# A decoder layer on one core: the first weight sum of the down projection moves ahead of its stage, its first split to the head of each chunk, and the last two token blocks close one by one

## The chip, the cores and the metric

The kernel runs on one core of one Trainium2 chip. The metric is the device time of one execution in microseconds (us), the median of several runs. TensorE is called PE, VectorE DVE, ScalarE ACT, GpSimd POOL and SyncE SP. SP and POOL are used here mainly as the two queues that issue transfers; only POOL's transfers add into their destination.

## The reference

One decoder layer over 512 tokens with a model width of 1024, all in float32. The change touches only the second half, the convolutional gated feed-forward network, and the projection just ahead of it:

```python
h = h + rmsnorm(merged @ w_out, mix_post_g)          # end of the mixer
xn = rmsnorm(h, ffn_pre_g)
hid = xn @ w_up                                      # 1024 -> 2 * 2816
conv = conv_b + sum_j shifted(hid, j) * conv_w[j]    # three taps along the sequence
a, u = split(conv, 2)
y = (gelu(a) * u) @ w_down                           # 2816 -> 1024
out = h + rmsnorm(y, ffn_post_g)
```

## The kernel before

**Precision.** Every float32 operand is split into a rounded high part and a low part (`split`, or `weights` for a matrix that comes from memory), and each product is three matmuls: high by high, high by low, low by high. `weights` issues a load on SP into a tile `wraw`, ACT makes the high part (line 98) and DVE the low part (line 99). The three tags `wraw`, `whi` and `wlo` have three buffers each, so at most three weight matrices are anywhere between their load and their last matmul. Up weights show in the trace as `h_wup` and `l_wup`, plain blocks of the down weights as `h_db` and `l_db`.

**Up projection.** The loop over `f` runs over the 22 blocks of 128 hidden channels. Each `f` has two weight matrices (the gate channel and the value channel), each with 24 matmuls of 512 columns into a PSUM bank of tag `acc`. `gate_up` then runs the convolution (ACT line 846, DVE line 848), the gelu and the gate, and prepares the operands of the down projection.

**Down projection.** It works in five chunks of 512 hidden channels, `c` 0 to 4; two more blocks of 128 remain and are multiplied plainly at the end (`close`). Chunk `c` is worked on during the up projection of `f = 4c+4` to `4c+7`. Within a chunk a 2 by 2 block product is done with seven block products in place of eight (Strassen's scheme with Winograd's sums). Four of its weight operands are sums of weight blocks, named t1 (T1 in the text), T2, T3 and T4 in the code, and three are plain blocks: b21, b11 and b22. A product over one block is 12 matmuls.

T1, T2 and T4 come out of one tile `dr`: SP loads block (0,1), POOL adds block (0,0), which gives T1. `parts` splits T1 into the pair `dht`, `dlt` (lines 853 and 854) and then has POOL add a further block into the same tile (line 910), which gives T2; splitting T2 starts the last addition, which gives T4. T3 has its own tile `dt`. Before the change `dr` has two buffers in the pool `ffn`, which opens after the mixer's pools have closed, and `sums` asks for both tiles at `f = 4c+2`.

**Order.** The program text is a list of priorities for the Tile framework: it lets an instruction go ahead of earlier ones on its engine when it counts it ready sooner and a buffer is free, and then fixes one order for each engine. At run time each engine and each queue keeps to its own order, and an instruction that waits holds up all that stand behind it on its engine. `steps` (chunks 0 to 3) and `last` (chunk 4) are generators: `go(cur)` runs one to its next `yield`, once ahead of the up matmuls of each `f` and once behind them. In the text before, the weights of chunk `c` are asked for in this order: up 4c+4 (two), b21, b11, up 4c+5 (two), T1, and so on.

**End.** The 512 tokens are four blocks `n` of 128, each with two column halves. `close(n, hf)` adds the two remaining blocks, `summed` adds the bank to the accumulator and starts the sum of squares, `finish(n)` computes the reciprocal root (POOL, `r2o`), scales, adds the residual and stores. Blocks 2 and 3 still lack the products S3·T3 and A22·T4 when blocks 0 and 1 are finished.

Of the kernel before, what the change touches and what calls it, by code (L numbers as in the profile page):

```python
# [9 lines left out]
F32 = mybir.dt.float32  # L10
# [3 lines left out]
ALU = mybir.AluOpType  # L14
PSUM = bass.MemoryType.PSUM

P = 128
S = 512
# [48 lines left out]
def hybrid_layer_kernel(ctx: ExitStack, tc: tile.TileContext, a):  # L67
    nc = tc.nc
# [144 lines left out]
    with ExitStack() as mix:  # L213
# [79 lines left out]
        for i in range(2):  # L293
            proj_fm(a["w_gq"][i], f"wgq{i}", lambda pq, i=i: nc.vector.scalar_tensor_tensor(
                out=gq[:, i, :], in0=pq, scalar=0.125, in1=rsb, op0=ALU.mult, op1=ALU.mult))
        for i in range(2):
            proj_fm(a["w_gk"][i], f"wgk{i}", lambda pk, i=i: nc.vector.tensor_tensor(
                out=gk[:, i, :], in0=pk, in1=rsb, op=ALU.mult))
# [40 lines left out]
        for gp in range(4):  # L339
# [4 lines left out]
            for gg in range(2):  # L344
                g = 2 * gp + gg
                c = slice(g * 64, (g + 1) * 64)
                nc.vector.scalar_tensor_tensor(
                    out=u_t[:, :, c], in0=sp[:, gg * 256:(gg + 1) * 256].rearrange("p (n d) -> p n d", d=64),
# [103 lines left out]
        for i in range(2):  # L452

            ups = [bank("att", f"up{i}{e}") for e in range(2)]
            for c in range(7):
                n, r = c // 2, (c % 2) * 64
# [245 lines left out]
        def gain(name):  # L702
            g = late.tile([P, D], F32, tag="gain", bufs=2, name=name)
            nc.gpsimd.dma_start(out=g, in_=a[name].broadcast_to([P, D]))
            nc.gpsimd.tensor_scalar(out=g, in0=g, scalar1=32.0, scalar2=1.0, op0=ALU.mult, op1=ALU.mult)
            return g
# [2 lines left out]
        nc.gpsimd.dma_start(out=cw, in_=a["ffn_conv_w"])  # L709
        cb = const.tile([P, 2 * KF], F32, name="cb")  # L710
        nc.gpsimd.dma_start(out=cb, in_=a["ffn_conv_b"])
        gpost = gain("mix_post_g")
        gpre = gain("ffn_pre_g")

        with tc.tile_pool(name="mlo", bufs=1, side="right") as mlp:
# [58 lines left out]
            def out_part(n, u, hf, w):  # L774
                hi, lo = w
                t = slice(n * P, (n + 1) * P)
                for j in range(2):
                    k = 2 * u + j
                    mm3(bs[n][hf], mh[:, k, t], ml[:, k, t], hi[:, j, :], lo[:, j, :], k == 0, k == KD - 1)
# [5 lines left out]
            for u in range(2):  # L785
                for hf in range(2):
                    w = weights(a["w_out"][u, hf], [2, S], f"wo{u}{hf}")
                    for n in range(NB):
                        out_part(n, u, hf, w)
            for hf in range(2):  # L790
                wo[2, hf] = weights(a["w_out"][2, hf], [2, S], f"wo2{hf}", (keep[0][:, hf], keep[1][:, hf]))
            for hf in range(2):
# [46 lines left out]
    NCH = 5  # L839
# [18 lines left out]
    def gate_up(f, pa, pu):  # L858
# [12 lines left out]
        if f % 2 == 0:  # L871
# [13 lines left out]
        nc.vector.scalar_tensor_tensor(out=l[:, S2, :], in0=sm[:, 3, :], scalar=-1.0,  # L885
                                       in1=h[:, S2, :].bitcast(F32), op0=ALU.mult, op1=ALU.subtract)

    class Down:


        def __init__(self, c):
            self.c, self.w = c, a["ffn_w_down"][c]
            self.bank = {}

        def sums(self):

            c, w = self.c, self.w
            self.r = ffn.tile([P, 2, S], F32, tag="dr", bufs=2, name=f"dr{c}")
            nc.sync.dma_start(out=self.r, in_=w[0, 1])
            nc.gpsimd.dma_start(out=self.r, in_=w[0, 0], accum_op=ALU.add)  # L900
            self.t3 = ffn.tile([P, 2, S], F32, tag="dt", bufs=1, name=f"dt{c}")
            nc.sync.dma_start(out=self.t3, in_=w[1, 1])
            nc.gpsimd.dma_start(out=self.t3, in_=w[0, 1], accum_op=ALU.add)

        def parts(self, x, name, then=None):
            hi = ffn.tile([P, 2, S], F32R, tag="dh", bufs=2, name=f"dh{name}{self.c}")
# [6 lines left out]
        def plain(self, r, s_, name):  # L913
            return weights(self.w[r, s_], [2, S], f"d{name}{self.c}")

        def product(self, tag, blk, w, start, stop):
            hi, lo = w
            for tau in range(2):
                key = (tag, tau)
                if start:  # L920
                    self.bank[key] = bank(tag, f"dn{tag}{self.c}{tau}")
                out = self.bank[key]
                t = slice(tau * P, (tau + 1) * P)
                for j in range(2):
                    h, l = halves[2 * self.c + j]
                    mm(out, h[:, blk, t], hi[:, j, :], start=start and j == 0, stop=False, skip_group_check=True)  # L926
                    mm(out, h[:, blk, t], lo[:, j, :], start=False, stop=False, skip_group_check=True)  # L927
                    mm(out, l[:, blk, t], hi[:, j, :], start=False, stop=stop and j == 1, skip_group_check=True)  # L928
# [8 lines left out]
                    nc.vector.tensor_tensor(out=dst, in0=src, in1=dst, op=ALU.add)  # L937

        def steps(self):
            b21 = self.plain(1, 0, "b21")  # L940
            yield
            self.product("tv", A12, b21, True, True)
            self.add("tv", 0, 0, True)
            b11 = self.plain(0, 0, "b11")
            yield
            t1 = self.parts(self.r, "t1", self.w[1, 1])
            yield
            self.product("att", A11, b11, True, False)
            self.add("att", 0, 0)
            self.add("att", 1, 0, True)  # L950
            self.product("att", S1, t1, False, False)
            self.add("att", 1, 1, True)
            yield
            T2, b22 = self.parts(self.r, "t2", self.w[1, 0]), self.plain(1, 1, "b22")
            yield
            self.product("tv", S2, T2, True, False)
            self.add("tv", 0, 1, True)
            self.product("att", S4, b22, False, True)
            self.add("att", 0, 1)
            yield  # L960
            T3, T4 = self.parts(self.t3, "t3"), self.parts(self.r, "t4")
            yield
            self.product("tv", S3, T3, False, False)
            self.add("tv", 1, 1)
            self.product("tv", A22, T4, False, True)
            self.add("tv", 1, 0)

        def last(self):

            b11 = self.plain(0, 0, "b11")  # L970
            yield
            self.product("att", A11, b11, True, False)
            self.add("att", 0, 0)
            self.add("att", 1, 0)
            t1 = self.parts(self.r, "t1", self.w[1, 1])
            yield
            T2 = self.parts(self.r, "t2", self.w[1, 0])
            yield
            self.product("att", S1, t1, False, False)
            self.add("att", 1, 1)  # L980
            self.product("tv", S2, T2, True, False)
            self.add("tv", 0, 1)
            b22, b21, T3 = self.plain(1, 1, "b22"), self.plain(1, 0, "b21"), self.parts(self.t3, "t3")
            yield
            self.product("att", S4, b22, False, False)
            self.product("acc", A12, b21, True, False)
            T4 = self.parts(self.r, "t4")
            yield
            self.product("tv", S3, T3, False, False)
            self.add("tv", 1, 1)  # L990
            self.product("tv", A22, T4, False, False)

    def go(it):
        next(it, None)
# [1 line left out]
    for f in range(2):  # L996
        gate_up(f, first_ps[f, 0], first_ps[f, 1])
    cur = None
    nxt = end = Down(0)
    for f in range(2, KF):  # L1000
        c, i = f // 4 - 1, f % 4
        if i == 0 and f >= 4:
            cur, nxt = (nxt.steps(), Down(c + 1)) if c + 1 < NCH else (nxt.last(), None)
        pair = []
        chs = [(ch, weights(a["ffn_w_up"][ch], [KD, P], f"wup{ch}")) for ch in (f, KF + f)]
        if cur:
            go(cur)
        if nxt and i == 2:
            nxt.sums()
            end = nxt  # L1010
        for ch, w in chs:
            pu = bank("acc", f"up{ch}_ps")
            up_part(pu, w, slice(0, S))
            pair.append(pu)
        if cur:
            go(cur)
        gate_up(f, *pair)
# [21 lines left out]
    def close(n, hf):  # L1039

        fresh = n >= 2 and hf == 1
        for k in range(2):
            t = slice(k * S + n * P, k * S + (n + 1) * P)
            hi, lo = ws[k][0][:, hf, :], ws[k][1][:, hf, :]
            mm(bs[n][hf], h[:, t], hi, start=fresh and k == 0, stop=False, skip_group_check=True)
            mm(bs[n][hf], h[:, t], lo, start=False, stop=False, skip_group_check=True)
            mm(bs[n][hf], l[:, t], hi, start=False, stop=k == 1, skip_group_check=True)
# [3 lines left out]
    def summed(n, hf):  # L1051
        y, o = acc[:, n, hf, :], t2(f"o{n}{hf}")
        if hf == 0:
            nc.vector.tensor_tensor(out=y, in0=bs[n][hf], in1=y, op=ALU.add)
        else:
            nc.vector.scalar_tensor_tensor(out=y, in0=bs[n][hf], scalar=-1.0, in1=y,
                                           op0=ALU.mult, op1=ALU.subtract)
        if n not in s2s:
            s2s[n] = small.tile([P, 2], F32, tag="s2", name=f"s2o{n}")
        nc.scalar.activation(bs[n][hf], y, AF.Square, accum_out=s2s[n][:, hf:hf + 1])  # L1060
        nc.vector.tensor_tensor(out=o, in0=y, in1=gffn[:, hf * S:(hf + 1) * S], op=ALU.mult)  # L1061
        outs[n, hf] = o
# [21 lines left out]
    for n in (2, 3):  # L1084
        close(n, 1)
    finish(1)
    for _ in cur:
        pass
    for n in (2, 3):
        summed(n, 1)  # L1090
    for n in (2, 3):
        close(n, 0)
        summed(n, 0)
        finish(n)


def _layouts(i):
# [52 lines left out]
```

## Time and profile before

| | |
|---|---|
| median of 3 runs | 856.19 us (856.06 to 856.78) |
| time of the profiled execution | 855.42 us |
| its span, first to last instruction | 853.7 us |
| mean granted clock of PE in it | 0.993 |
| PE busy share of the span | 98% |
| DVE, ACT, POOL busy share | 66%, 45%, 12% |

The profile is one execution. Its time lies 0.77 us under the median, and 1.7 us of it lie around the span. PE's busy share counts a matmul that is slow as busy, so it has to be read beside the granted clock. In the timeline the time in brackets is how long the engine was idle before the instruction, with what released it.

### The profile page before, as it was taken

What the parts mean: (1) busy time and instruction counts of PE and PEld (TensorE: products, weight loads), DVE (VectorE), ACT (ScalarE), POOL (GpSimd) and SP (SyncE); (2) the same over time, 40 slices, a digit from 0 to 9 for tenths busy, and PEclk for the clock granted to TensorE, in tenths of its full rate; (3) what the DMA queues carried; (4) which work ended last, traced back from release to release, by engine and by line L of the source; (5) the groups of instructions that cost most, each with busy time, mean ns of one, the idle gap of its engine ahead of it and who ended that gap; (6) DMA issues with size and microseconds to landing.
All of it is one profiled execution on the core that took longest, in us unless ns stands there. A gap on an engine that the chain in (4) does not pass through costs nothing. (4 is left out here: it accounts for less than half of the span.)

```text
span 853.7 us, 10478 instructions
## 1 busy us (share of the span) xinstructions
PE 836.3 (98%) x3945; PEld 685.2 (80%) x3945; DVE 564.4 (66%) x810; ACT 382.3 (45%) x584; POOL 103.5 (12%) x161
## 2 busy tenths in 40 slices
PE   9999999999999999999999999899999999999995
PEld 6778878888888888888888898688788788788884
DVE  5468344544368888785574856765886886886886
ACT  7545323332356556553244534554444444444442
POOL 2210003100012231332000101000000000000101
PEclk9999999999999999999999999899999999999998
DMA  8622322223232222226335028436536536534502
GB/s 305 227 75 74 98 75 75 72 77 99 99 100 74 75 74 75 75 75 244 101 118 179 1 76 221 125 117 178 122 117 168 136 123 169 127 126 122 145 28 99
DMA packets 30226, 99.57 MB, mean 117 GB/s; under 512 B 3664, under 2 KB 4160, under 8 KB 30176
## 3 DMA queue, kind: packets, MB, share of 16 engines
q1 hardware_dynamic: 25776, 83.97, 29.5%
q0 software_dynamic: 4400, 14.94, 8.9%
q8 instruction: 31, 0.51, 0.3%
q14 instruction: 19, 0.16, 0.1%
HBM read 96.80 MB, written 2.10 MB: 116 GB/s over the span
## 5 line engine op out<-in xcount | busy, mean ns | idle before, releaser
L816 PE MATMUL up_ps<-hTh,h_wup 128*128 128x512 f32 (+1 forms) x336 | 130.2, 388 | 4.2 <-ACT h_wup L98 4.2
L818 PE MATMUL up_ps<-hTh,l_wup 128*128 128x512 f32 (+1 forms) x336 | 130.5, 388 | 1.4 <-DVE l_wup L99 1.4
L817 PE MATMUL up_ps<-hTl,h_wup 128*128 128x512 f32 (+1 forms) x336 | 130.1, 387 | 0.0
L99 DVE TENSOR_TENSOR l_wup<-r_wup,h_wup 128x1024 fp32r<-128x1024 f32 x41 | 50.1, 1221 | 45.7 <-ACT h_wup L98 45.2
L816 PEld LDWEIGHTS up_ps<-hTh,h_wup 128*128 128x128 f32 x336 | 63.7, 190 | 17.4 <-ACT h_wup L98 5.0
L168 PE MATMUL wg_ps<-xTh,h_wg 128*128 128x512 f32 x192 | 77.6, 404 | 0.0
L818 PEld LDWEIGHTS up_ps<-hTh,l_wup 128*128 128x128 f32 x336 | 63.7, 189 | 15.9 <-DVE l_wup L99 3.4
L170 PE MATMUL wg_ps<-xTh,l_wg 128*128 128x512 f32 x192 | 75.2, 392 | 0.0
L169 PE MATMUL wg_ps<-xTl,h_wg 128*128 128x512 f32 x192 | 75.0, 391 | 0.0
L817 PEld LDWEIGHTS up_ps<-hTl,h_wup 128*128 128x128 f32 x336 | 63.7, 190 | 12.7
L848 DVE SCALAR_TENSOR_TENSOR cv<-up_ps,cw,cv 128x511 f32<-128x511 f32 (+1 forms) x88 | 65.3, 743 | 11.9 <-ACT cv L846 11.2
L98 ACT ACTIVATE h_wup<-r_wup 128x1024 fp32r<-128x1024 f32 x41 | 43.3, 1056 | 45.4 <-PE up_ps L817 35.8
L98 ACT ACTIVATE h_wg<-r_wg 128x1024 fp32r<-128x1024 f32 x24 | 25.5, 1061 | 46.0 <-PE wg_ps L169 29.3
L170 PEld LDWEIGHTS wg_ps<-xTh,l_wg 128*128 128x128 f32 x192 | 36.0, 188 | 8.1
L168 PEld LDWEIGHTS wg_ps<-xTh,h_wg 128*128 128x128 f32 x192 | 36.2, 188 | 7.1 <-issue 0.5
L169 PEld LDWEIGHTS wg_ps<-xTl,h_wg 128*128 128x128 f32 x192 | 36.2, 188 | 6.4
L612 DVE TENSOR_TENSOR_SCAN re<-re 128x128 f32<-128x128 f32 (+3 forms) x32 | 27.5, 860 | 15.2 <-POOL re L609 14.8
L99 DVE TENSOR_TENSOR l_wg<-r_wg,h_wg 128x1024 fp32r<-128x1024 f32 x24 | 32.6, 1357 | 6.9 <-ACT h_wg L98 6.9
L846 ACT ACTIVATE cv<-up_ps,cb,cw 128x512 f32<-128x512 f32 x44 | 33.5, 762 | 5.0 <-PE up_ps L818 4.7
L404 DVE TENSOR_TENSOR gl<-wg_ps,rsb 128x512 f32<-128x512 f32 x24 | 16.4, 682 | 26.8 <-PE wg_ps L170 26.8
L860 ACT ACTIVATE cv<-cv 128x512 f32<-128x512 f32 x22 | 13.9, 632 | 42.5 <-DVE cv L848 42.5
L609 POOL TENSOR_SCALAR_AFFINE_SELECT re<-re 128x128 f32<-128x128 f32 x32 | 12.9, 404 | 161.1 <-ACT re L606 148.7
(496 smaller groups left out, 2009.5 us busy)
## 6 DMA issues: line engine op xcount, KB each, us to landing
r_wup<-in_ffn_w_up SPq DMA_DIRECT2D x44, 512.0 KB, 3.3
r_wg<-in_w_gate SPq DMA_DIRECT2D x24, 512.0 KB, 3.3
dr<-in_ffn_w_down POOLq DMA_DIRECT2D x15, 512.0 KB, 5.4
r_db<-in_ffn_w_down SPq DMA_DIRECT2D x15, 512.0 KB, 3.4
r_wo<-in_w_out SPq DMA_DIRECT2D x8, 512.0 KB, 3.3
dr<-in_ffn_w_down SPq DMA_DIRECT2D x5, 512.0 KB, 4.6
dt<-in_ffn_w_down SPq DMA_DIRECT2D x5, 512.0 KB, 3.4
dt<-in_ffn_w_down POOLq DMA_DIRECT2D x5, 512.0 KB, 7.0
```

The source lines that it names most:

```text
L98: nc.scalar.activation(hi[:, p], raw[:, p], AF.Copy)
L99: nc.vector.tensor_tensor(out=lo[:, p], in0=raw[:, p], in1=hi[:, p].bitcast(F32), op=ALU.subtract)
L168: mm(out, hi[:, k, :], xTh[:, k, :], start=k == 0, stop=False)
L169: mm(out, hi[:, k, :], xTl[:, k, :], start=False, stop=False)
L170: mm(out, lo[:, k, :], xTh[:, k, :], start=False, stop=k == KD - 1)
L404: nc.vector.tensor_tensor(out=gl[0][:, j, :], in0=pg, in1=rsb, op=ALU.mult)
L612: nc.vector.tensor_tensor_scan(out=rev, data0=rev, data1=rev, initial=1.0, op0=ALU.mult, op1=ALU.bypass)
L816: mm(pu[:, t], hi[:, k, :], hTh[:, k, t], start=k == 0, stop=False, skip_group_check=True)
L817: mm(pu[:, t], hi[:, k, :], hTl[:, k, t], start=False, stop=False, skip_group_check=True)
L818: mm(pu[:, t], lo[:, k, :], hTh[:, k, t], start=False, stop=k == KD - 1, skip_group_check=True)
L846: nc.scalar.activation(o, pu, AF.Identity, bias=cb[:, c:c + 1], scale=cw[:, c, 2:3])
L848: nc.vector.scalar_tensor_tensor(out=o[:, j:], in0=pu[:, :S - j], scalar=cw[:, c, 2 - j:3 - j], in1=o[:, j:], op0=ALU.mult, op1=ALU.add)
```

## The change

It has four parts. The sum T1 of chunk 0 gets its tile in the pool `late`, which is open during the output projection, and is asked for there; the other chunks' `dr` tiles alternate between `ffn` and `late`, one buffer each. The request for `dt` moves from the third to the fourth `f` of a group. In `steps` and `last` the split of T1 (with the addition that it starts) moves to the head, ahead of b21 (b11 in `last`), and in `steps` the request for b11 moves one step back, behind both up weights of the next `f`. At the end A22·T4 is done for token block 2 first, block 2 is closed and finished, and then the same for block 3.

```diff
+        def sum_r(c, pool):
+            r = pool.tile([P, 2, S], F32, tag="dr", bufs=1, name=f"dr{c}")
+            nc.sync.dma_start(out=r, in_=a["ffn_w_down"][c, 0, 1])
+            nc.gpsimd.dma_start(out=r, in_=a["ffn_w_down"][c, 0, 0], accum_op=ALU.add)
+            sums[c] = r
...
                     for n in range(NB):
                         out_part(n, u, hf, w)
+            sum_r(0, late)
...
+    def sum_t3(c):
+        t3s[c] = ffn.tile([P, 2, S], F32, tag="dt", bufs=1, name=f"dt{c}")
+        nc.sync.dma_start(out=t3s[c], in_=a["ffn_w_down"][c, 1, 1])
+        nc.gpsimd.dma_start(out=t3s[c], in_=a["ffn_w_down"][c, 0, 1], accum_op=ALU.add)
...
         def steps(self):
-            b21 = self.plain(1, 0, "b21")
+            t1, b21 = self.parts(self.r, "t1", self.w[1, 1]), self.plain(1, 0, "b21")
             yield
             self.product("tv", A12, b21, True, True)
             self.add("tv", 0, 0, True)
+            yield
             b11 = self.plain(0, 0, "b11")
-            yield
-            t1 = self.parts(self.r, "t1", self.w[1, 1])
             yield
...
         def last(self):
-            b11 = self.plain(0, 0, "b11")
+            t1, b11 = self.parts(self.r, "t1", self.w[1, 1]), self.plain(0, 0, "b11")
             yield
             self.product("att", A11, b11, True, False)
             self.add("att", 0, 0)
             self.add("att", 1, 0)
-            t1 = self.parts(self.r, "t1", self.w[1, 1])
             yield
...
-            self.product("tv", A22, T4, False, False)
+            for tau in range(2):
+                self.product("tv", A22, T4, False, False, (tau,))
+                yield
...
-        if nxt and i == 2:
-            nxt.sums()
-            end = nxt
+        if i == 2 and 0 <= c < NCH - 1:
+            sum_r(c + 1, late if c % 2 else ffn)
+        if i == 3 and c < NCH - 1:
+            sum_t3(c + 1)
...
-    for _ in cur:
-        pass
+    go(cur)
     for n in (2, 3):
         summed(n, 1)
-    for n in (2, 3):
-        close(n, 0)
-        summed(n, 0)
-        finish(n)
+    close(2, 0)
+    summed(2, 0)
+    finish(2)
+    go(cur)
+    close(3, 0)
+    summed(3, 0)
+    finish(3)
```

## Rows read from the trace of the kernel before

**Rows 1.** Page, parts 1 and 2: PE's busy time; clock in 40 slices

```profile
PE 836.3 (98%) x3945; PEld 685.2 (80%) x3945; DVE 564.4 (66%) x810; ACT 382.3 (45%) x584; POOL 103.5 (12%) x161
...
PEclk9999999999999999999999999899999999999998
```

**Rows 2.** Waits of PE: for whom; us in total, times, longest

```profile
PE up_ps L816 <- ACT h_wup L98: 4.2, 1, 4.2
PE up_ps L818 <- DVE l_wup L99: 1.4, 3, 0.5
```

**Rows 3.** Windows from one b21 product to the next (the last to b11)

```profile
541.96:612.40 70.44, 66.24 (x278) 53.10 (x276) 48.53 (x67) 34.85 (x48) 2.59 (x3) 0.95 0.46 128
612.40:676.03 63.63, 63.11 (x277) 51.49 (x276) 48.67 (x69) 27.84 (x35) 3.45 (x4) 1.00 0.54 141
676.03:739.46 63.43, 63.09 (x278) 51.57 (x276) 48.16 (x68) 27.85 (x35) 3.45 (x4) 1.00 0.54 141
739.46:803.17 63.71, 63.18 (x277) 51.50 (x276) 48.67 (x68) 27.84 (x35) 3.15 (x4) 1.00 0.46 131
```

**Rows 4.** Chain that ended last, 800 to 854: first, last of 128 pieces

```profile
799.93 0.23 PE up_ps L816
...
828.95 0.24 PE dnacc L1047
```

**Rows 5.** The same chain, 500 to 552: start, us, what

```profile
522.78 8.52 DMA dr<-in_ffn_w_down
...
549.27 0.79 PE up_ps L816
550.06 0.43 PE up_ps L817
```

**Rows 6.** ACT's timeline, 460 to 560: conversions and splits in its order

```profile
514.96 1.06 ACT L98 ACTIVATE h_wup<-r_wup 128x1024 fp32r<-128x1024 f32 x1 [0.21 <-PE up_ps L817]
...
520.16 1.06 ACT L853 ACTIVATE dht<-dr 128x1024 fp32r<-128x1024 f32 x1 [2.43 <-DMA dr<-in_ffn_w_down]
...
531.32 1.06 ACT L853 ACTIVATE dht<-dr 128x1024 fp32r<-128x1024 f32 x1 [7.45 <-DMA dr<-in_ffn_w_down]
...
532.59 1.04 ACT L98 ACTIVATE h_wup<-r_wup 128x1024 fp32r<-128x1024 f32 x1
...
542.93 1.04 ACT L98 ACTIVATE h_db<-r_db 128x1024 fp32r<-128x1024 f32 x1
...
548.18 1.04 ACT L98 ACTIVATE h_wup<-r_wup 128x1024 fp32r<-128x1024 f32 x1
```

**Rows 7.** POOL's timeline: first and last of four additions into tiles

```profile
514.76 0.94 POOL L900 DMA_DIRECT2D dr<-in_ffn_w_down  x1 [23.19 <-ACT sh L853]
...
522.78 0.87 POOL L910 DMA_DIRECT2D dr<-in_ffn_w_down  x1 [3.80 <-DVE dlt L854]
```

**Rows 8.** Transfers, 508 to 532: POOL's queue; packets, MB, share

```profile
q0 software_dynamic: 576, 2.10, 48.2%
```

**Rows 9.** SP's timeline, 505 to 540: loads of b21 and b11, then up

```profile
517.31 7.32 SPq L97 DMA_DIRECT2D r_db<-in_ffn_w_down  x2
535.13 4.71 SPq L97 DMA_DIRECT2D r_wup<-in_ffn_w_up  x2
```

**Rows 10.** ACT's timeline in chunk 1, 606 to 616

```profile
607.01 1.05 ACT L98 ACTIVATE h_db<-r_db 128x1024 fp32r<-128x1024 f32 x1
...
613.94 1.04 ACT L98 ACTIVATE h_wup<-r_wup 128x1024 fp32r<-128x1024 f32 x1
```

**Rows 11.** DVE's timeline at the end, blocks 2 and 3

```profile
843.28 0.69 DVE L1054 TENSOR_TENSOR acc<-dntv,acc 128x512 f32<-128x512 f32 x1 [1.26 <-PE dntv L1047]
...
846.50 1.41 DVE L1074 SCALAR_TENSOR_TENSOR o<-o,r2o,hx 128x512 f32<-128x512 f32 x2 [0.44 <-POOL r2o L190]
...
848.76 1.54 DVE L1074 SCALAR_TENSOR_TENSOR o<-o,r2o,hx 128x512 f32<-128x512 f32 x3 [0.73 <-POOL r2o L190]
```

**Rows 12.** POOL's timeline during the output projection

```profile
466.89 0.57 POOL L190 TENSOR_TENSOR r2y<-v2y,expo 128x1 f32<-128x1 f32 x1 [60.49 <-DVE v2y L732]
```

More of the change, by code (lines that the diff above doesn't have):

```diff
@@ L711, in hybrid_layer_kernel @@
         nc.gpsimd.dma_start(out=cb, in_=a["ffn_conv_b"])
+        sums = {}
+        def sum_r(c, pool):
[3 more added lines that the diff above has]
+            sums[c] = r
         gpost = gain("mix_post_g")
@@ L886, in gate_up @@
                                        in1=h[:, S2, :].bitcast(F32), op0=ALU.mult, op1=ALU.subtract)
+    t3s = {}
+    def sum_t3(c):
+        t3s[c] = ffn.tile([P, 2, S], F32, tag="dt", bufs=1, name=f"dt{c}")
+        nc.sync.dma_start(out=t3s[c], in_=a["ffn_w_down"][c, 1, 1])
+        nc.gpsimd.dma_start(out=t3s[c], in_=a["ffn_w_down"][c, 0, 1], accum_op=ALU.add)
     class Down:
@@ L893, in __init__ @@
             self.bank = {}
[L895 to L903, printed above, removed]
+            self.r, self.t3 = sums.pop(c), t3s.pop(c)
         def parts(self, x, name, then=None):
@@ L914, in plain, with product @@
             return weights(self.w[r, s_], [2, S], f"d{name}{self.c}")
-        def product(self, tag, blk, w, start, stop):
+        def product(self, tag, blk, w, start, stop, taus=(0, 1)):
             hi, lo = w
-            for tau in range(2):
+            for tau in taus:
                 key = (tag, tau)
@@ L998, in hybrid_layer_kernel @@
     cur = None
-    nxt = end = Down(0)
     for f in range(2, KF):
@@ L1002, in hybrid_layer_kernel @@
         if i == 0 and f >= 4:
-            cur, nxt = (nxt.steps(), Down(c + 1)) if c + 1 < NCH else (nxt.last(), None)
+            end = Down(c)
+            cur = end.steps() if c + 1 < NCH else end.last()
         pair = []
```

## The prediction

> **What bounds the kernel now.** I read the page first, then PE's waits, then windows over the chunks of the down projection, and only then the chain and the engines' timelines around the one place that stood out. On the page PE is busy 98% of the span and its clock is full in every slice but one [rows 1]: the kernel is bound by its matmuls, and an edit that adds or removes none can only win back the places where PE stands still or runs slowly. The waits say how little of that there is: one wait of 4.2 us for the high part of an up weight, and three of together 1.4 us for the low part of another [rows 2].
>
> The windows put a price on both. Each runs from the start of one chunk's b21 product to the next chunk's (the last to b11), and each holds the same 276 matmuls: 8 up matrices of 24 and 7 products of 12. They last 70.44, 63.63, 63.43 and 63.71 us [rows 3]. What they would last unhindered comes from the chain near the end, where 128 matmuls follow each other without a gap from 799.93 to 828.95 [rows 4]: 29.02 / 128 = 0.2267 us each, times 276 = 62.57 us. So the four windows lose 7.87, 1.06, 0.86 and 1.14 us. Chunk 0 is the outlier, and its loss is more than its 4.2 us of idling: behind the gap a matmul takes 0.43 us where 0.23 is usual [rows 4, 5], the granted clock having fallen to 1.2 GHz after PE stood still. That part is 7.87, less the 4.2 of the gap, less the 1.02 that the other chunks lose on average: 2.65 us.
>
> Why chunk 0 is late, the chain says: it goes back from PE's restart at 549.27 to an addition into `dr`, issued at 522.78 and 8.52 us on its way [rows 5]. That is T2. ACT has T2's split in its order right ahead of the conversion of an up weight and stands still for 7.45 us until 531.32 [rows 6]. All the convolutions, gates and conversions behind it come late, DVE, which needs ACT's results, as well. The reader is to see two things in ACT's rows. First, T1 was late already (2.43 us of waiting, split at 520.16), so T2 could not be asked for sooner. Second, at 542.93 ACT converts b11, and only at 548.18 the up weight that PE has been waiting for [rows 6]. Both orders are what the diff changes.
>
> **Chunk 0, the order of the buffers.** I number up matrices by `f`, a and b. From the b21 product at 541.96 [rows 3] backwards at 24 x 0.2267 = 5.44 us each, PE needs 4b at 536.5, 4a at 531.1 and 3b at 525.6; forwards, 5a at 541.96 + 12 x 0.2267 = 544.7. Three buffers hold the high parts, in the order 4a, 4b, b21, b11, 5a, 5b before. So 5a gets 4b's buffer, free at 541.96, 2.7 us ahead of need. With b11 behind 5b, 5a gets 4a's, free at 536.5: 8.2 us ahead. The load moves too: b11's was the second of two issues that end at 524.6, 5a's came at 535.13 [rows 9]; now 5a takes the earlier place. Even if ACT were as late as before, a conversion of 5a in b11's place would end at 542.93 + 1.04 = 543.97 [rows 6], ahead of 544.7, and the low part would follow about as long after. b11, whose product follows both matrices of 5, has some 11 us more than that.
>
> **Chunk 0, the sum.** T1 is summed during the output projection, so it can be split as soon as the pool `ffn` opens at about 510. Before, four additions ran through POOL's queue from 514.76 until T2 landed at 531.30, 2.10 MB with hardly a pause [rows 5, 7, 8]: 16.5 / 4 = 4.1 us each. Now three are left there (T2, the next chunk's T1, T3). If T2 goes first it lands near 513 + 4.1 = 517; if last, at 514.76 + 3 x 4.1 = 527.1. I take the late end, since POOL keeps to its order and the request for T3 stands ahead in the text. ACT then still waits for T2, but while only up products run and each buffer is free 11 us ahead of need: two splits and conversions of 1.06 us [rows 6] after 527.1 bring 4a's high part at 529.2, before 531.1. For the catching up I leave 0.5 us (0 to 5.3 us: a 2.65 us gap and as much again for the clock). A page of the Trainium skill, "DMA: Bandwidth & Descriptors", section "Anatomy of one DMA — SWDGE (gpsimd) path", gives 2.0 us plus the bytes over 436 GB/s for such a transfer, by estimate 3.2 us for 512 KB; the row has 8.52, so I go by the row, and by the page T2 would be in time for everything and the 0.5 would be 0.
>
> What goes with it: of chunk 0's 7.87 us I count on 7.3, as the other chunks lose 0.55 us each beside their waits (3.06 in all, less the 1.4 of the waits [rows 2, 3], over three). Bounds: 0, if the order stays, and 7.87.
>
> **Chunks 1 to 3.** In chunk 1 the same pattern stands, only milder: b11 is converted at 607.01, the up weight behind b21 at 613.94 [rows 10]. With b11 behind, that weight's buffer is free 5.4 us sooner. I take the 1.4 us of the three waits; bounds 0 and all 3.06 us. T1's split at the head changes nothing I can price: the tile is filled a chunk ahead and the addition behind it only starts earlier. Without that cover ACT would wait there as it does for T2 now. Chunk 4 has no such wait in PE's list, so 0.
>
> **What the moved steps cost.** One load on SP and one addition on POOL go to the output projection, where POOL has been idle for 60.49 us before its next instruction at 466.89 [rows 12]: that is the cover, and without it the reciprocal root there would wait up to 8.5 us (T2's landing is the longest I have). On SP the load stands ahead of the last output weights, whose three buffers hide it. `dt` one `f` later and the alternation of the `dr` tiles move no transfer that something waits for. All this at 0.
>
> **The end.** PE's last matmul stays where it is. Six matmuls of A22·T4 (1.36 us) move behind block 2's close, so block 2's add, which found DVE idle for 1.26 us at 843.28, starts up to that much sooner, and its root and two scales with it [rows 11]. Block 3's scales at 848.76 waited for a root that stood behind block 2's scales. Gain 0 if DVE's order keeps them so, 1.26 if all of it comes through; I take half, 0.6.
>
> **Sum.** 7.3 + 1.4 + 0.6 - 0.5 = 8.8 us. The profiled execution goes from 855.42 to 846.6; on the median, 0.77 us above it, 856.19 - 8.8 = 847.4 us.
>
> **Rivals.**
> *The stall moves.* T2's wait comes earlier on ACT and delays 4a or 4b by 2 to 3 us, and the clock falls with it: 3 to 5 us of the gain go. For it: DVE and ACT still have the same work in that stretch. Against: the buffers' lead is largest there. 856.19 - 8.8 + 4 = about 851.
>
> *The change does not do what it says.* The text is only a list of priorities; b11 or T2 could come out in the old place. Then only the end and the small waits give way: 856.19 - 2.0 = 854.2.
>
> *Slower.* T2's addition is asked for so early that its split lands on ACT ahead of 3b's conversion, which stood at 514.96 [rows 6] and is needed at 525.6. If T2 lands at X, 3b's high part is there at X + 2.1; PE idles X - 523.5 and loses a further 2.65 us to the clock. Against the 9.3 us of gains this decides from X = 530.2; at 531.3, T2's landing before, the result is 857.3, and each later us adds one. Against it: one addition fewer in the queue. A rule of the Trainium skill speaks for it ("SBUF — State Buffer", section "SBUF: two separate sides"): DVE and POOL share a port pair that is held exclusively, and POOL's transfers starve while some DVE work holds it; DVE is busy two thirds of the time [rows 1]. The trace has little of that: POOL's issue at 514.76 took 0.94 us against 0.87 later [rows 7].
>
> **Chances.** Forecast 0.62; the stall moves 0.18; undone 0.08; gains and new waits cancel 0.06; slower 0.06. What a measurement here can tell from no change is about 0.2%, 1.7 us. So faster 0.87 (most of the third case included), same 0.07, slower 0.06. The range goes from all bounds at their best, 856.19 - 10.9 - 1.3 = 844.0, less what is unlikely to come off at once (844.4), up to the moved stall with its clock (852.0).
>
> **What would show it.** Right: no PE wait of microseconds at b21's end in chunk 0, clock full throughout, the first window near 63.2 us and the others near 63.0, the 5a conversion ahead of b11's on ACT, T2 landing before 527, block 2's add near 842. Wrong: ACT's idle time before T2's split as long as now and a PE gap behind it; a PE wait in the output projection for `h_wo` or `h_wup`; POOL's first root there late.

## The result, and the profile after

| | before | after |
|---|---|---|
| median | 856.12 us (856.02 to 856.78, 4 runs) | 845.07 us (844.65 to 845.42, 4 runs) |
| profiled execution, span | 855.42, 853.7 us | 844.95, 843.2 us |
| mean granted clock of PE | 0.993 | 0.998 |

The ratio is 0.9869, with a 95% interval of 0.9852 to 0.9886: 11.05 us gained where 8.8 were forecast. The time lies inside the predicted range.

The page of the changed kernel, PE's busy time and the granted clock, against [rows 1]:

```profile
PE 832.1 (99%) x3945; PEld 684.8 (81%) x3945; DVE 564.5 (67%) x810; ACT 382.5 (45%) x584; POOL 104.2 (12%) x161
...
PEclk9999999999999999999999999999999999999999
```

PE does the same 3945 matmuls, and the slice with the low clock is gone. All of PE's waits in the changed kernel (for whom; us in total, times, longest), against [rows 2]:

```profile
PE warm_ps L114 <- POOL warm L109: 1.4, 1, 1.4
PE wu_ps L103 <- ACT h_wu L98: 0.5, 1, 0.5
PE wt L624 <- ACT be L607: 0.3, 2, 0.2
PE up_ps L826 <- ACT hTh L776: 0.2, 1, 0.2
```

The up products no longer wait for a weight, neither for the 4.2 us in chunk 0 nor for the three half microseconds behind it. The windows of the changed kernel from one b21 product to the next (the last to b11), against [rows 3] (length; busy time of PE, PEld, DVE, ACT, POOL; clock, DMA share, GB/s):

```profile
542.21:605.01 62.80, 62.80 (x277) 51.65 (x276) 46.00 (x62) 32.81 (x45) 2.57 (x3) 1.00 0.52 143
605.01:667.78 62.77, 62.77 (x278) 51.66 (x276) 48.91 (x69) 27.75 (x35) 3.45 (x4) 1.00 0.52 143
667.78:730.54 62.76, 62.76 (x277) 51.65 (x276) 48.06 (x67) 27.93 (x35) 3.45 (x4) 1.00 0.53 143
730.54:793.31 62.77, 62.77 (x277) 51.66 (x276) 48.79 (x69) 27.75 (x35) 3.98 (x5) 1.00 0.48 134
```

They are 7.64, 0.86, 0.67 and 0.94 us shorter than [rows 3], and PE is busy in each from edge to edge. From the end of the last window to the end of the span it was 50.53 us (803.17 to 853.70) and is 49.89 (793.31 to 843.20): 0.64 less. The first b21 product starts at 542.21 and not at 541.96, 0.25 later. So the spans differ by 7.64 + 2.47 + 0.64 - 0.25 = 10.5 us, which is 853.7 less 843.2.

ACT's timeline of the changed kernel around chunk 0's b21 (start, us; in brackets the idle time before), against [rows 6]. In order: T1, T2, 4a, 4b, 5a, b11 (4a to 5a are up weights, numbered as in the prediction).

```profile
511.18 1.05 ACT L863 ACTIVATE dht<-dr 128x1024 fp32r<-128x1024 f32 x1
...
524.83 1.06 ACT L863 ACTIVATE dht<-dr 128x1024 fp32r<-128x1024 f32 x1 [5.07 <-DMA dr<-in_ffn_w_down]
...
526.98 1.04 ACT L98 ACTIVATE h_wup<-r_wup 128x1024 fp32r<-128x1024 f32 x1
...
530.69 1.04 ACT L98 ACTIVATE h_wup<-r_wup 128x1024 fp32r<-128x1024 f32 x1
...
542.22 1.05 ACT L98 ACTIVATE h_wup<-r_wup 128x1024 fp32r<-128x1024 f32 x1
...
547.16 1.07 ACT L98 ACTIVATE h_db<-r_db 128x1024 fp32r<-128x1024 f32 x1
```

T1 is split at 511.18 (520.16 before), T2 at 524.83 (531.32), and 5a is converted at 542.22 (548.18), now ahead of b11. ACT still stands still for 5.07 us for T2; this idling lies where PE has a lead. The low part of 5a follows on DVE, and POOL's queue shows three additions, in the order T3, T2 and the next chunk's T1, where [rows 7] has four. The two timelines of the changed kernel, DVE's and POOL's:

```profile
543.88 1.22 DVE L99 TENSOR_TENSOR l_wup<-r_wup,h_wup 128x1024 fp32r<-128x1024 f32 x1
```
```profile
514.85 0.93 POOL L903 DMA_DIRECT2D dt<-in_ffn_w_down  x1 [23.03 <-DMA dt<-in_ffn_w_down]
516.01 0.86 POOL L918 DMA_DIRECT2D dr<-in_ffn_w_down  x1 [0.23 <-issue]
516.75 1.01 POOL L718 DMA_DIRECT2D dr<-in_ffn_w_down  x1
```

5a's product begins 12 matmuls behind 542.21, at 544.92, and its third matmul, the first that reads the low part, at 545.38. The low part is done at 543.88 + 1.22 = 545.10. So the changed kernel has 0.28 us to spare here; the experiments will come back to this number.

In chunk 1 the order on ACT is turned round as well (timeline, against [rows 10]): the up weight behind b21 at 599.63, b11 at 608.23.

```profile
599.63 1.04 ACT L98 ACTIVATE h_wup<-r_wup 128x1024 fp32r<-128x1024 f32 x1
...
608.23 1.05 ACT L98 ACTIVATE h_db<-r_db 128x1024 fp32r<-128x1024 f32 x1
```

The end on DVE (timeline, against [rows 11]): block 2's add, block 3's add, block 3's scales.

```profile
832.08 0.68 DVE L1063 TENSOR_TENSOR acc<-dntv,acc 128x512 f32<-128x512 f32 x1
...
835.83 0.68 DVE L1063 TENSOR_TENSOR acc<-dntv,acc 128x512 f32<-128x512 f32 x1
...
838.25 1.54 DVE L1083 SCALAR_TENSOR_TENSOR o<-o,r2o,hx 128x512 f32<-128x512 f32 x3 [0.72 <-POOL r2o L190]
```

Block 2's add has no idle time before it any more. Block 3's last scales still follow its root.

### The profile page after: what moved, and what is told of

The parts are those of the page before. It is cut to its first block, busy times and chain, and to the rows that moved or that the text cites. A ratio compares the mean times of both kernels' runs of the same rounds, so it can differ in the third digit from the quotient of the medians.

```text
span 843.2 us, 10475 instructions
## 1 busy us (share of the span) xinstructions
PE 832.1 (99%) x3945; PEld 684.8 (81%) x3945; DVE 564.5 (67%) x810; ACT 382.5 (45%) x584; POOL 104.2 (12%) x161
## 4 chain that ended last, share of the span: by engine, by line
PE 91%; issue 4%; DVE 3%; POOL 1%; ACT 1%; DMA 0%; POOLq 0%; DVEq 0%; SPq 0%; ACTq 0%
PE up_ps L826 10%; PE up_ps L828 10%; PE up_ps L827 10%; PE wg_ps L168 5%; PE wg_ps L170 5%; PE wg_ps L169 5%; PE pp L103 3%; PE pp L105 3%; PE pp L104 3%; PE dntv L934 2%; PE dntv L936 2%; PE dntv L935 2%; PE wo L104 2%; PE wo L105 2%; PE wo L103 2%
```

## The experiments

The theory going in: 5a is late because T2's split and b11's conversion stand ahead of it on ACT, and each part of the change takes one of them away. Rivals: one part does it all; the buffer order is what counts, or ACT's order; the place of the request or of the split counts, not the sum's buffer.

### One part alone

`e1_b11_only`: the kernel before with b11 asked for one step later, nothing else.

```diff
             self.add("tv", 0, 0, True)
-            b11 = self.plain(0, 0, "b11")
             yield
+            b11 = self.plain(0, 0, "b11")
             t1 = self.parts(self.r, "t1", self.w[1, 1])
```

> The kernel before with one part of the change alone: b11 is asked for behind both up weights of the next f (chunks 0 to 3); the sum stays in its stage, T1's split and the end stay as they were. My theory: either of two edits is enough for the big gap in chunk 0. With b11 behind, the up weight 5a gets its buffer 8.2 us ahead of need, so it is ready even though T2 lands as late as before (about 531). Expected 846 to 848 us (7.6 of chunk 0 less up to 1, and 2.5 of chunks 1 to 3), ACT still waiting 7 us for T2, no PE wait of microseconds. Rival: the late T2 is the cause, and b11's place cures only the three small waits: 853.5 us, with the 4.2 us wait still there.

Measured: 847.94 us (847.53 to 848.57), ratio 0.9904 [0.9888, 0.9921]. Of 11 us this one line brings 8.2. Its PE waits, its first two windows, and its T2 and 5a on ACT:

```profile
PE up_ps L818 <- DVE l_wup L99: 1.1, 1, 1.1
...
PE up_ps L816 <- ACT h_wup L98: 0.2, 1, 0.2
```
```profile
542.34:607.01 64.67, 63.38 (x278) 51.50 (x276) 48.05 (x66) 34.53 (x47) 2.60 (x3) 1.00 0.49 139
607.01:669.79 62.78, 62.78 (x277) 51.66 (x276) 48.47 (x68) 27.75 (x35) 3.46 (x4) 1.00 0.52 143
```
```profile
531.29 1.06 ACT L853 ACTIVATE dht<-dr 128x1024 fp32r<-128x1024 f32 x1 [6.77 <-DMA dr<-in_ffn_w_down]
...
544.30 1.05 ACT L98 ACTIVATE h_wup<-r_wup 128x1024 fp32r<-128x1024 f32 x1
```

T2 is as late as before, and PE still waits for only 1.3 us. The rival, a wait of 4.2 us that stays, falls. From chunk 1 on the windows (62.78, 62.75, 62.74) are already those of the changed kernel.

`e2_sum_only`: the changed kernel with b11 back in its old place and the old end; `e11_sum_only_again`: the same text, run again.

```diff
-            yield
             b11 = self.plain(0, 0, "b11")
             yield
+            yield
...
-            for tau in range(2):
-                self.product("tv", A22, T4, False, False, (tau,))
-                yield
+            self.product("tv", A22, T4, False, False)
```

> The change without b11's new place and without the new end: the first sum during the output projection, the split of T1 at the head. My theory: T2 lands near 525, chunk 0 then loses what the other chunks lose (about 1 us), and the small waits of chunks 1 to 3 stay: 849 to 850 us, PE's waits for a low part now four of about 0.5 us. Rival: the buffer order is what counts, 5a still waits behind b11: a gap of over 2 us in chunk 0 and 852 us or more.

> Run 2 once more, for a second profile: its times ran from 851.3 to 855.6, and its profile was the fastest of them. My theory: PE's gap ahead of 5a is just about as long as the clock stands (2.0 us in that profile), so executions differ by whether the clock falls: a profile at 853 us or more shows a longer gap, a half-speed stretch behind it, or both. Rival: the difference lies elsewhere, spread over the span, and the gap is the same.

Measured: 853.2 us (851.3 to 855.55, 12 runs), ratio 0.9968 [0.9956, 0.998], and the second time 853.43 (852.41 to 854.18), 0.997 [0.9958, 0.9981]. The sum alone brings 2.7 us by the ratio; my expectation of 849 to 850 us fell, and the rival held (a gap of 2.0 us ahead of 5a, and over 852 us). The first run's T2, b11 and 5a on ACT, its PE waits and its first two windows; then the second run's T2 and 5a, its longest PE wait and first window:

```profile
524.73 1.06 ACT L863 ACTIVATE dht<-dr 128x1024 fp32r<-128x1024 f32 x1 [5.03 <-DMA dr<-in_ffn_w_down]
...
540.72 1.05 ACT L98 ACTIVATE h_db<-r_db 128x1024 fp32r<-128x1024 f32 x1
545.96 1.04 ACT L98 ACTIVATE h_wup<-r_wup 128x1024 fp32r<-128x1024 f32 x1
```
```profile
PE up_ps L828 <- DVE l_wup L99: 2.1, 4, 0.5
PE up_ps L826 <- ACT h_wup L98: 2.0, 1, 2.0
```
```profile
542.15:608.10 65.95, 63.40 (x278) 51.49 (x277) 46.34 (x62) 32.77 (x45) 2.57 (x3) 1.00 0.49 136
608.10:671.75 63.65, 63.12 (x277) 51.51 (x276) 48.40 (x68) 27.86 (x35) 3.46 (x4) 1.00 0.52 141
```
```profile
526.12 1.06 ACT L863 ACTIVATE dht<-dr 128x1024 fp32r<-128x1024 f32 x1 [6.18 <-DMA dr<-in_ffn_w_down]
...
547.36 1.04 ACT L98 ACTIVATE h_wup<-r_wup 128x1024 fp32r<-128x1024 f32 x1
```
```profile
PE up_ps L826 <- ACT h_wup L98: 3.2, 1, 3.2
```
```profile
542.39:610.93 68.54, 64.83 (x278) 0.98 0.47 131
```

T2 lands as early as in the changed kernel, yet 5a comes 3.7 us later, behind b11. In the second run, whose profiled execution is 2.9 us longer (854.18 against 851.3), T2 came 1.39 us later and 5a 1.40 us later; PE's gap is longer and its window's clock 0.98. So the two edits are not equal: b11's place alone takes most of chunk 0's gap, the sum alone does not. Chunks 1 to 3 gain nothing here (63.65, 63.71, 63.60).

### Buffer or engine order

`e5_own_buffers`: the kernel before with b11 in its old place in the text, but in a high and a low buffer of its own (one scratch buffer less makes the room).

```diff
...
-            b11 = self.plain(0, 0, "b11")
+            b11 = self.plain(0, 0, "b11", own=True)
...
```

> The kernel before, with b11 in its old place in the text, but with a pair of buffers of its own for its high and low part, so that it takes none from the three that the up weights share (to make room, the pool of 512-column scratch tiles has 8 in place of 9 buffers). My theory: what counts is which buffer the up weight 5a has to wait for. It now gets 4a's, as with b11 behind, so the gap and the small waits go although b11 is loaded and converted ahead of 5a and T2 lands at 531: 847 to 849 us. Rival: what counts is that ACT, DVE and SP do b11's work ahead of 5a's; then the gap of 4 us stays, 854 us or more.

Measured: 849.45 us (848.71 to 850.54), ratio 0.9919 [0.99, 0.9937]: a little above the expected range, and far below the rival's 854. Taking b11 out of the shared buffers also frees chunk 1 of its wait (the second window lasts 62.75). Its ACT timeline from T2 on (`ownh` is b11), and the longest of PE's waits for an operand:

```profile
533.32 1.06 ACT L853 ACTIVATE dht<-dr 128x1024 fp32r<-128x1024 f32 x1 [7.88 <-DMA dr<-in_ffn_w_down]
...
536.21 1.05 ACT L98 ACTIVATE ownh<-r_db 128x1024 fp32r<-128x1024 f32 x1
...
547.34 1.05 ACT L98 ACTIVATE h_wup<-r_wup 128x1024 fp32r<-128x1024 f32 x1
```
```profile
545.39 0.50 PE L928 MATMUL dntv<-h_db,sh 128*128 128x512 f32 x1 [2.10 <-ACT sh L853]
```

b11's conversion is still ahead of 5a's and now ahead of b21's too. T2 landed latest of all runs here, 2.0 us behind `e1_b11_only`. Both push back the split of an activation (`sh`) that b21's product reads, and PE waits 2.1 us for it. So the shared buffers are most of b11's part (by the ratios 6.9 of 8.2 us). As for the rest, from T2's split to 5a's conversion it is 14.02 us here and 13.01 in `e1_b11_only`: b11's place on ACT is worth about 1.0 us, the later T2 about 2.0.

### What the home sum is worth, and by what

By the home sum I mean chunk 0's T1 summed early, in the pool `late`. `e4_no_home` takes away the request in the output projection (the tile stays in `late`); `e6_not_home` swaps the pools as well, so that chunk 0's sum is in `ffn` again and chunk 1's in `late`; `e7_old_split` is the changed kernel with T1's split in its old place in the text. The first diff is that of `e6_not_home`, the second that of `e7_old_split`.

```diff
-            sum_r(0, late)
...
-        if i == 2 and 0 <= c < NCH - 1:
-            sum_r(c + 1, late if c % 2 else ffn)
+        if i == 2 and c < NCH - 1:
+            sum_r(c + 1, ffn if c % 2 else late)
```
```diff
-            t1, b21 = self.parts(self.r, "t1", self.w[1, 1]), self.plain(1, 0, "b21")
+            b21 = self.plain(1, 0, "b21")
...
             b11 = self.plain(0, 0, "b11")
+            t1 = self.parts(self.r, "t1", self.w[1, 1])
```

> The whole change less the sum during the output projection: chunk 0's tile dr is still in the pool late, but is asked for at f = 2 as before. My theory (b11's place is enough): within 1 us of the whole change, 845 to 846 us. Rival (the early sum is what removed the gap): T2 lands near 531 again and the gap with its slow clock comes back, 852 us or more. Should the framework load it early by itself, since the tile's pool is open, the run says nothing on this.

> The whole change, but chunk 0's tile dr lies in the pool that opens after the output projection (the next chunk's lies in the other). Run 3 did not undo this part, the tile being loaded early wherever it is asked for. My theory: the early sum is worth what run 1 lacks beside the end, 847.9 - 0.8 - 845.1 = about 2 us: 847 us, T2 landing at 527 or later and a PE wait of about 1 us for the low part of 5a. Rival: with b11's place the early sum is worth nothing: 845.1 us.

> The whole change with T1's split back at its old place in the text of chunks 0 to 3. My theory: the framework lets the split go ahead as soon as its tile is there, so its place gives nothing: 845.1 us, the same order on ACT and the same 5 us wait for T2. Rival: the split comes later, T2 is asked for later and a PE wait comes back: 846 us or more.

Measured: 845.07 (844.76 to 845.38), ratio 0.9869 [0.985, 0.9887]; 845.02 (844.54 to 846.17), 0.987 [0.9849, 0.989]; 845.62 (845.32 to 846.98), 0.988 [0.9862, 0.9899]. None differs from the changed kernel by more than runs scatter. In the first the framework put the load at 392.59 by itself (392.69 in the changed kernel): the open pool decides, not the line. In the third ACT, DVE and POOL have the same order in this stretch as in the changed kernel, so T1's split goes to the head without its line. The second tells most. Its T1 and T2 on ACT, and its 5a; then POOL's request for T2 in it; then POOL's requests for the next chunk's T1 and for T2 in `e1_b11_only`:

```profile
520.39 1.06 ACT L862 ACTIVATE dht<-dr 128x1024 fp32r<-128x1024 f32 x1 [2.52 <-DMA dr<-in_ffn_w_down]
...
528.38 1.06 ACT L862 ACTIVATE dht<-dr 128x1024 fp32r<-128x1024 f32 x1 [4.28 <-DMA dr<-in_ffn_w_down]
...
541.41 1.05 ACT L98 ACTIVATE h_wup<-r_wup 128x1024 fp32r<-128x1024 f32 x1
```
```profile
523.01 0.86 POOL L917 DMA_DIRECT2D dr<-in_ffn_w_down  x1 [5.63 <-DVE dlt L863]
```
```profile
518.47 0.86 POOL L900 DMA_DIRECT2D dr<-in_ffn_w_down  x1 [0.57 <-DMA dr<-in_ffn_w_down]
523.43 0.87 POOL L910 DMA_DIRECT2D dr<-in_ffn_w_down  x1 [4.10 <-DVE dlt L854]
```

T1 is as late as before and the time is that of the changed kernel. In this run and in `e1_b11_only` ACT has the same order, and POOL asks for T2 at nearly the same time, 523.01 and 523.43; it is split at 528.38 in the one and 531.29 in the other. What stands between them in POOL's queue is the next chunk's T1, issued at 518.47 in `e1_b11_only` and, as its tile lies in `late`, at 396.11 here. My expectation of a loss fell.

`e7_old_split` also shows how thin the margin is. Its profiled execution is one of two long ones among its five (846.94 us): POOL issued the additions 2.1 us later (516.92), T2 was split at 526.92, 5a converted at 544.32, and PE waited 1.1 us for its low part.

```profile
526.92 1.06 ACT L863 ACTIVATE dht<-dr 128x1024 fp32r<-128x1024 f32 x1 [7.24 <-DMA dr<-in_ffn_w_down]
...
544.32 1.05 ACT L98 ACTIVATE h_wup<-r_wup 128x1024 fp32r<-128x1024 f32 x1
```

### The end

`e3_old_end`: the changed kernel with the old end (the second half of the diff of `e2_sum_only`, and blocks 2 and 3 closed in one loop). `e8_scales_last` and `e9_scales_last_r2`: block 2's scales made to stand behind block 3's add, with a small extra tile, in a tag of its own (r3) in the first and in the old tag r2 in the second; the first diff is that of `e8_scales_last`. `e10_moved_only`: the changed kernel with block 3's root in a tag of its own, which moves addresses and nothing else.

```diff
         r = small.tile([P, 1], F32, tag="r2", name=f"r2o{n}")
         rsqrt(r, v)
+        if after is not None:
+            after()
+            late_r = small.tile([P, 1], F32, tag="r3", bufs=1, name=f"r3o{n}")
+            nc.vector.scalar_tensor_tensor(out=late_r, in0=acc[:, 3, 0, 0:1], scalar=0.0, in1=r,
+                                           op0=ALU.mult, op1=ALU.add)
+            r = late_r
...
```
```diff
-        r = small.tile([P, 1], F32, tag="r2", name=f"r2o{n}")
+        r = small.tile([P, 1], F32, tag="r3" if n == 3 else "r2", name=f"r2o{n}")
```

> The change with the old end: A22 T4 for both token blocks, then both closed and finished. My theory: the stretch from the last b11 product to the end was 0.64 us shorter with the change (50.53 against 49.89), so 0.6 us slower than the whole change, 845.7 us. Rival: the end gives nothing by itself, 845.1 us.

> The whole change, and block 2's two scales at the end are held back behind block 3's add, by one small DVE instruction that reads block 3's result times zero. In the changed kernel block 3's add waited about 1.3 us behind these scales. My theory: block 3's chain starts 1.3 us sooner, less 0.2 for the small instruction and what the scales then delay: 844.2 us (0.5 to 1 us less). Rival: the scales now stand ahead of block 3's root or its scales and take it back: 845.1 us.

> Run 8 without its new buffer: the held-back scales take their factor from the ring of small tiles that is there already, so no pool is one tile larger and nothing behind it moves in SBUF. In run 8 the end was 0.7 us shorter (5.6 to 4.9 us from PE's last matmul to DVE's last instruction), but every matmul of the down products with plain blocks took 396 ns in place of 389. My theory: that came with the moved addresses, and without them the end's gain is seen: 844.4 us. Rival: run 8 was slow for a reason in its order, and this one takes 847 to 848 us too.

> The changed kernel, with one thing different: block 3's reciprocal root has a tag of its own in the pool of small tiles, so this pool is one tile larger and the pools opened after it lie a little further on. The order on all engines is the same. My theory: the moved addresses alone cost what run 8 lost, 847 to 848 us, with the plain blocks' matmuls at 396 ns. Rival: 845.1 us, 389 ns.

Measured: `e3_old_end` 845.84 (845.8 to 845.85), 0.9878 [0.9859, 0.9896], so by the medians the new end gives 0.77 us. Its profiled execution shows where: from the end of the last window it takes 50.54 us, 0.65 more than the changed kernel. But it also has a wait of 0.4 us for 5a's low part (its first window lasts 63.48), so not all of the 0.77 need be the end's. `e8_scales_last` 847.88 (847.06 to 848.58), 0.9899 [0.9881, 0.9917], slower than the changed kernel. `e9_scales_last_r2` 845.2 (844.01 to 846.55), 0.9877 [0.9858, 0.9895], not to be told from it. `e10_moved_only` 846.65 (846.3 to 848.21), 0.9898 [0.9877, 0.9918]. The matmuls of b21 by its high part in the last three kernels (groups of instructions; ns: least, median, most), `e8`, `e9` and `e10` in turn:

```profile
L934 PE MATMUL dntv<-h_db,sh x16: 392/395/396, 543.0 to 734.5; 128*128 128x512 f32 x16
```
```profile
L934 PE MATMUL dntv<-h_db,sh x16: 389/389/390, 541.8 to 732.3; 128*128 128x512 f32 x16
```
```profile
L934 PE MATMUL dntv<-h_db,sh x16: 392/392/392, 543.0 to 734.1; 128*128 128x512 f32 x16
```

The changed kernel has 389 here. `e8_scales_last` and `e9_scales_last_r2` have the same order; the first, with the new tag, has the slower matmuls and is 2.7 us slower by the medians, 1.9 by the ratios to the kernel before that ran beside each. b21's matmuls are only the sample that shows it: PE's busy time as a whole is 835.0 us in `e8_scales_last` and 833.7 in `e10_moved_only`, against 832.1 in the changed kernel and 831.9 in `e9_scales_last_r2`. So it is the placement that costs, and not the order. The profiled execution of the second has a span of 842.3 us, 0.9 less than the changed kernel's, but the medians don't bear this out. None of the runs clearly beats the changed kernel.

## Why the prediction was right, and where its sizes were off

**One relation holds over the runs.** The time from T2's split to 5a's conversion on ACT depends on the order alone: runs with the same order around chunk 0 agree within 0.02 us. The latest harmless T2 follows. 5a's third matmul reads its low part and starts 3.17 us behind the first b21 matmul where nothing waits. The low part is done 2.9 us behind the start of 5a's conversion (2.3 where b11 stands ahead of 5a, since DVE is waiting for it there). With b21 at 542.2, 5a may then start at 542.5 (543.1), and T2 at that less the distance. The sixth column is measured: how much more than 3.17 us behind the first b21 matmul 5a's third matmul starts.

| kernel | T2 | 5a | distance | latest T2 | third matmul late by | first window less 62.80 |
|---|---|---|---|---|---|---|
| before [rows 3, 6] | 531.32 | 548.18 | 16.86 | 526.2 | 5.40 | 7.64 |
| `e1_b11_only` | 531.29 | 544.30 | 13.01 | 529.5 | 1.73 | 1.87 |
| `e6_not_home` | 528.38 | 541.41 | 13.03 | 529.5 | 0 | 0.05 |
| `e2_sum_only` | 524.73 | 545.96 | 21.23 | 521.9 | 3.00 | 3.15 |
| `e11_sum_only_again` | 526.12 | 547.36 | 21.24 | 521.9 | 4.15 | 5.74 |
| `e7_old_split` | 526.92 | 544.32 | 17.40 | 525.1 | 1.65 | 1.85 |
| `e3_old_end` | 525.13 | 542.52 | 17.39 | 525.1 | 0.53 | 0.68 |
| `e5_own_buffers` | 533.32 | 547.34 | 14.02 | 528.5 | 4.84 | 4.96 |
| after | 524.83 | 542.22 | 17.39 | 525.1 | 0 | 0 |

b11 ahead of 5a costs 3.85 us (16.86 against 13.01, 21.23 against 17.39). Where T1 comes home, T2 is split ahead of 4a and not behind it, which lengthens the distance by 4.4 us while T2 comes 6.5 us sooner. In five of the seven late rows the window loses 0.12 to 0.20 us more than the third matmul is late. In the other two, before and `e11_sum_only_again`, it loses 2.24 and 1.59 more: there PE's granted clock fell behind the pause ahead of 5a. In `e5_own_buffers` it fell too, but behind b21's pause, and PE was waiting for 5a's low part again when it had risen.

The margin of the changed kernel, 0.28 us, is smaller than the spread of T2 between runs of one order (524.83, 525.13, 526.92). That the profiled execution shows no wait at 5a at all is partly luck.

**Chunk 0, the order of the buffers: right, with less to spare than said.** 5a got ahead of b11. "Even if ACT were as late as before" is `e1_b11_only`: the high part was 0.2 us late where the sum had it 0.7 early, and PE waited 1.1 us more for the low part, so 1.87 us of the gain still needed T2. The step that was off is "in b11's place": ACT put two activations ahead, so 5a's conversion started at 544.30 and not at 542.93, and the low part took 1.8 us behind it.

**Chunk 0, the sum: the price right, the early split one of two ways.** T2 landed before 527 (524.8). The sum counted three additions at 4.1 us each, the last of them at 527.1; T3, T2 and the next chunk's T1 landed 5.5, 8.8 and 10.5 us behind their issues, at 520.4, 524.8 and 527.3, with T2 the second. T2 came sooner in the changed kernel because it was asked for sooner: T1's split, 9.0 us earlier, brought its issue from 522.78 to 516.01, and it was 8.8 us under way, against 8.5 before. But T1 need not be early: `e6_not_home` has T1 at 520.39 and the full gain. There T2 is asked for as late as before and is 5.4 us under way, against 7.9 in `e1_b11_only`, with one addition fewer ahead of it, and its order gives T2 4.4 us more time. The 7.3 us came to 7.64. The estimate of 3.2 us from the Trainium skill ("DMA: Bandwidth & Descriptors", section "Anatomy of one DMA — SWDGE (gpsimd) path") is short of both 5.4 and 8.8, in each of which an earlier addition was still under way at the start, and the measurements decide.

**Chunks 1 to 3: the mis-sized term.** I took the 1.4 us of the three waits; the windows gave 2.47. A wait costs more than its length: the windows of `e2_sum_only` with one wait of 0.5 us last 63.65, those of `e1_b11_only` without it 62.78. The matmuls right behind the wait show it (PE's timeline of `e2_sum_only`; start, us):

```profile
611.98 0.50 PE L828 MATMUL up_ps<-hTh,l_wup 128*128 128x512 f32 x1 [0.53 <-DVE l_wup L99]
612.32 0.40 PE L826 MATMUL up_ps<-hTh,h_wup 128*128 128x512 f32 x1
612.56 0.40 PE L827 MATMUL up_ps<-hTl,h_wup 128*128 128x512 f32 x1
```

The first takes 0.34 us of PE's time and the next 0.24, against 0.2275 in an undisturbed window (62.80 / 276). Why they are slower no run shows. The prediction left 0.55 us to each window beside its wait; 0.36 of it went with the wait, and 0.2 was no loss at all, as an undisturbed window takes 62.77 us and not the 62.57 that it reckoned from the matmuls near the end. The gain lies between my value and the upper bound of 3.06.

**The moved steps: 0, right.** SP's load of the last gate weights, which stands ahead of the early sum's load, starts at 389.97 before and at 390.21 after; the first b21 product follows 151.99 and 152.00 us later. The early sum in between costs PE nothing. It ran sooner than predicted, and not under the cover that the prediction named: SP's load is at 392.69 and POOL's addition at 396.43, ahead of the output projection, whose first matmul is at 438.1. POOL's next instruction began at 405.50 in place of 403.79, and PE waited for none of this.

**The end: 0.6, measured 0.64 in the trace, and 0.65 (by the medians 0.77) in `e3_old_end`.**

**The reserve of 0.5 us for catching up was not needed.** The profiled executions differ by 10.47 us, 1.67 more than the 8.8 of the sum: 1.07 of chunks 1 to 3, 0.34 of chunk 0, the 0.5 and 0.04 of the end, less the 0.25 by which the first b21 product starts later, are 1.70. The medians differ by a further 0.58.

**The rivals.** The moved stall came, as ACT's 5.07 us ahead of T2, but 4a and 4b are there in time, and at 5a it ends 0.28 us short of PE; the profiled executions of `e3_old_end` and `e7_old_split` are beyond that line. The undone change did not come: the orders changed as the text asked. For the slower one T2's split would have had to stand ahead of 3b's conversion and T2 to land behind 530.2; 3b was converted at 515.21, ahead of the split, and T2 landed at 524.8. The rule that spoke for it, of the port that DVE and POOL share (the Trainium skill, "SBUF — State Buffer", section "SBUF: two separate sides"), is not seen in the length of POOL's issues, 0.86 to 1.01 us in that stretch. Whether it has a part in the 8.8 us that T2 was under way, no run here shows.

Two things were not tried: four shared weight buffers, and both sums (of chunk 0 and chunk 1) made early. Why the order has T2 ahead of 4a in the changed kernel, and 4a ahead of T2 in `e6_not_home`, was read from the traces and not tested.

## What to carry to other kernels

Ask of a rotating buffer who has it next, and give it to the operand that is needed soonest: one moved line that put a late-needed weight behind two early ones brought 8.2 of 11 us. Of a wait that lies behind a chain of work on another engine, measure the distance between the two ends; if it is fixed, it says how late the first may be, and what each order is worth. When a transfer is late, count what stands ahead of it in its queue before moving what starts it, and price a short wait of PE by the window, not by its length.

## What was unexpected of the hardware

- A tile in a tag of its own, which moves addresses in SBUF and leaves the order as it was, slowed b21's matmuls from 389 to 392 ns, raised PE's busy time from 832.1 to 833.7 us and the median by 1.6 us (`e10_moved_only`); in `e8_scales_last` those matmuls took 395, in `e9_scales_last_r2` with the old tags 389. By what the addresses act was not found.
- A 0.5 us wait of PE lengthened its window by 0.9 us, with the granted clock at 1.00.
- PE's pause of 2.0 us in `e2_sum_only` left the granted clock at 1.00 in its window; one of 2.1 us in `e5_own_buffers` stands in a window of 0.97, one of 3.2 in `e11_sum_only_again` in one of 0.98, and the 4.2 us before the change in one of 0.95. What decides it, these four pauses do not show.
